# Transfers in written order, later stores, earlier weights and a ring of three for conv results in an input projection

## The chip, the cores and the metric

The kernel runs on one core of one Trainium2 chip. The metric is the device time of one execution in microseconds (us). The same executable is run three times for a median, and one more execution is profiled. Smaller is better. The engines are TensorE (PE, and PEld for its weight loads), VectorE (DVE), ScalarE (ACT), GpSimd (POOL) and SyncE (SP), which issues most of the transfers here.

## The reference

One step of a layer with two kinds of heads. 2048 prompt tokens and 8 x 8 sampled tokens go through one input projection, then through forgetting attention (8 heads of 64) and an mLSTM matrix memory (4 heads of 128), one output projection and an MLP. All is float32.

```python
z = jnp.einsum('bsd,dc->bsc', x, w_in)            # (tokens, 1024) x (1024, 3600)
fq, fk, fv, ff = ...                              # 512, 512, 512 and 8 columns of z
flogf = log_sigmoid(ff + b_fox_f)
xpad = concatenate([conv_prev, z_qk], axis=1)     # 1024 columns, mLSTM's q and k
conv = conv_b + sum(xpad[:, j:j + S] * conv_w[j] for j in range(4))
qk = silu(conv)
mv, ig, lf, og = ...                              # 512, 4, 4 and 512 columns
...
# forgetting attention: prompt over itself, sampled tokens over a paged cache
s = q . k * scale + L_q - L_k                     # L: running sum of flogf
fox_h = softmax(s) @ v
# mLSTM: chunks with a carried state C, n, m
num = (W * (q . k)) @ v + (q @ C) * a
h = num / max(|nq|, exp(-m_t))
C = g * C + sum(w_key * k * v)
...
mix = concatenate([fox_h, norm(h) * mlstm_norm_w * og]) @ w_o
x1 = layer_norm(ALPHA * x + mix)
y = layer_norm(ALPHA * x1 + square(relu(x1 @ w1)) @ w2)
```

Keys, values and log forget values of all tokens, the mLSTM's states and the conv's history are outputs too.

## The kernel before

A float32 product is made of three matmuls of split operands: high part by high, high by low, low by high (`mm3`, L144 to L149). `split_hi` (L138) makes the high part on ACT and `split_lo` (L141) the low part on DVE.

The work has four stages: the input projection (to about 1004 us) with the mLSTM and the beginning of sampled attention beside it, prompt attention (`phase_b`, L838), the output projection, and the MLP. Sampled attention goes on beside all of them.

The projection (`block_a`, L404) goes over four blocks of 512 prompt tokens; block 0 also carries the 64 sampled tokens as tile 16. A block is 14 passes over 256 columns of `w_in`: two for mLSTM's v (with the gates' 16 columns in the second), four for the conv's q and k (loop over j, L438, two j a pass), two for the output gate, and two each for attention's q, k and v. A pass is made of four units (five in block 0 where token tiles are rows of the result), each of 24 matmuls into one of four accumulators (`pm`). `wload` (L221) loads and splits a pass's weights in two halves (raw `wra`, two buffers; `whi` and `wlo`, four each). `load_x` (L256) loads one tile of 128 tokens (`xn`, two buffers), turns it on PE (L271) and splits it.

In the conv loop ACT copies two accumulators into `qi` (L456, two buffers, three columns of history in front), DVE makes four taps into `ac` (L462 and L464), ACT takes the tanh into `th` (L466), DVE combines both into `th` (L467), and SP stores `th` to `dqk` (L468). `ac`, `th` and the queries' `qst` (L522) share a ring of three buffers. Other results are copied by ACT into `st` (four buffers, L423) and stored: `dv` L429, `dog` L501, keys L536, values L541; the queries `dq` L523.

After every unit `tick` is called with an estimate of the unit's time (2.6 us, or a hundredth of the columns). It adds this to two accounts and, as they pass PACE_M (2.3) and PACE_A (7.5), advances generators, which emit a piece of other work and yield:

- `gate_stream` (L284): gates of the block's tokens, then `rowset` (L328), running sums and maxima along rows on DVE, with rows turned on PE (`mr`, L325) and stored to `dnl`, `dM`, `dar` and `dgs`.
- the prologue of sampled attention: the page table's load (L1249), four groups of cached log forget values, each of eight scans (L1301), a small matmul, eight adds (`rx`, L1311) and stores to `dR`.
- `m_block` (L606) and `m_sample` (L686): the mLSTM's chunks; `m_load_qk` (L590) loads q and k from `dqk`, the products are L631, and `norm_out` and `turn` (L553 to L574) normalise a chunk's result `hh` and store it to `dmix`. `m_sample` loads the sampled states (`C0`, L748; its matmul is L755).
- `step` (L1548) of sampled attention: `k_gather` (L1376, an indirect transfer by POOL into `kT`), `k_turn` (L1382, transposes on DVE), `r_load` (L1389, `Rb` from `dR`), `qk_step` (32 small matmuls, L1405, and a DVE reduction L1412 with `Rb`), and every 32 steps `softmax` (L1424).

The program is written in one order, and the framework places instructions on each engine's queue by its own estimates of when they are ready. Two things restrict it: the dependencies and buffers, and `issue_after`, which keeps an instruction behind a named one; `beside` (L111) uses it so that work beside the projection isn't put ahead of the projection's last issued split or matmul. SP's transfers are issued in the order in which the framework places them; a transfer that waits holds up those behind it.

The lines that block 0 and the later blocks run through:

```python
for bi in range(4):
    g = block_a(bi)
    next(g)                                   # up to the end of the conv passes
    if bi == 0 and gen:
        macc[1].append(prologue(gen))
    macc[1].append(m_block(bi))
    for _ in g:
        pass
    if bi == 0:
        while macc[1] and "pro" not in mst:
            tick(PACE_M)
        acc[1] = gen                          # sampled attention's steps
        macc[1].append(m_sample())
```

Of the kernel before, what the change touches and what calls it, by code (L numbers as in the profile page):

```python
# [24 lines left out]
D = 1024  # L25
# [25 lines left out]

@with_exitstack
def body(ctx, tc, I, O, stages):
    nc = tc.nc
    V, A, G, T, SY = nc.vector, nc.scalar, nc.gpsimd, nc.tensor, nc.sync
# [61 lines left out]

    def tick(us):

        macc[0] += us  # L120
        while macc[1] and macc[0] > PACE_M:
            macc[0] -= PACE_M
            if beside(macc[1][0]) == 0:
                macc[1].pop(0)
        if not macc[1]:
            macc[0] = 0.0
        acc[0] += us
        while acc[1] is not None and acc[0] > acc[2]:
            acc[0] -= acc[2]
            if beside(acc[1]) == 0:  # L130
                acc[1] = None
# [57 lines left out]
    def conv_setup():  # L189
        cwn = pa.tile([5, 1024], F32, name="cwn", tag="xn", bufs=2)  # L190
        SY.dma_start(cwn[0:4], I["conv_w"][0])
        SY.dma_start(cwn[4:5], I["conv_b"])
        pcw = ppa.tile([128, 8, 5], F32, name="px", tag="pm", bufs=4)
# [3 lines left out]
        scn = pa.tile([24, 1024], F32, name="scn", tag="xn", bufs=2)  # L197
        SY.dma_start(scn, I["state_conv"][0].rearrange("b j c -> (b j) c"))
# [4 lines left out]
        SY.dma_start(bog, dap(I["b_og"], 0, [[0, 128], [1, 512]]))  # L203
        SY.dma_start(nwh, dap(I["mlstm_norm_w"], 0, [[0, 128], [1, 512]]))
        V.tensor_scalar(nwh, nwh, 0.5, None, op0=OP.mult)
        SY.dma_start(smT, I["state_m"][0].rearrange("b h -> h b"))
        SY.dma_start(gbias[:, 0:8], dap(I["b_fox_f"], 0, [[0, 128], [1, 8]]))
        SY.dma_start(gbias[:, 8:12], dap(I["b_ig"], 0, [[0, 128], [1, 4]]))
        SY.dma_start(gbias[:, 12:16], dap(I["b_fg"], 0, [[0, 128], [1, 4]]))
# [11 lines left out]
    def wload(cols):  # L221

        n = sum(c[1] for c in cols)
        H, L = [], []
        for kg in range(2):
            wr = pa.tile([128, 4 * 272], F32, name="wra", bufs=2)[:, :4 * n].rearrange("p (k c) -> p k c", k=4)
            o = 0
            for c0, m in cols:
                SY.dma_start(wr[:, :, o:o + m], w_in[kg * 512:(kg + 1) * 512, c0:c0 + m].rearrange("(k p) c -> p k c", p=128))
                o += m  # L230
            wh = pa.tile([128, 4 * 272], F32R, name="whi", bufs=4)[:, :4 * n].rearrange("p (k c) -> p k c", k=4)
            wl = pa.tile([128, 4 * 272], F32R, name="wlo", bufs=4)[:, :4 * n].rearrange("p (k c) -> p k c", k=4)
            split_hi(wh, wr)
            split_lo(wl, wr, wh)
            H += [wh[:, k] for k in range(4)]
            L += [wl[:, k] for k in range(4)]
        return H, L
# [18 lines left out]
    def load_x(bi, tiles):  # L256

        blk, pre, off = geom(bi)
        for t in tiles:
            i = int(off[t] >= pre + 256)  # L260
            if len(xT.setdefault(bi, [])) == i:
                w = 256 if i else 320
                xT[bi].append((pa.tile([128, 8, w], F32R, name=f"xh{i}"), pa.tile([128, 8, w], F32R, name=f"xl{i}")))
            n = tok_n(t)
            xn = pa.tile([128, D], F32, name="xn", bufs=2)
            SY.dma_start(xn[:n], x_of(t))
            (xh, xl), s = xcol(bi, t)
            for hf in range(2):
                px = ppa.tile([128, 4, 128], F32, name="px", tag="pm", bufs=4)
                for k in range(4):  # L270
                    T.transpose(px[:, k, :n], xn[:n, (hf * 4 + k) * 128:(hf * 4 + k + 1) * 128], ident[:n, :n])  # L271
                dh = xh[:, hf * 4:hf * 4 + 4, s]
                split_hi(dh, px[:, :, :n])
                split_lo(xl[:, hf * 4:hf * 4 + 4, s], px[:, :, :n], dh)
# [9 lines left out]
    def gate_stream(bi):  # L284
# [4 lines left out]
        def gates(z, lg, shape, bb):  # L289
# [21 lines left out]
            for a, b in zip(fs, fd):  # L311
# [4 lines left out]
        SY.dma_start(O["logf_prompt"][0, 0, t0:t0 + 512].rearrange("(c p) h -> p c h", p=128),  # L316
                     gnat[:, c0:c0 + 4, 0:8])
        if pre:
            gates(gats, gnats, [64, 16], gbias[:64])
            SY.dma_start(O["logf_sample"].rearrange("l b t h -> (l b t) h"), gnats[:, 0:8])  # L320
# [7 lines left out]
        def rowset(cols, base, n_el, np_, sample):  # L328
# [35 lines left out]
            SY.dma_start(dM[:, base:base + n_el], lr)  # L364
# [12 lines left out]
            SY.dma_start(dar[:, base:base + n_el], br)  # L377
            ge = pa.tile([4, 8], F32, name="ge", bufs=1)[:, :n_el // cl]
            V.tensor_copy(ge, br.rearrange("p (c t) -> p c t", t=cl)[:, :, cl - 1])
            if sample:  # L380
                SY.dma_start(dgs_s, ge)
                me = pa.tile([4, 8], F32, name="me", bufs=1)
                V.tensor_copy(me, mr.rearrange("p (c t) -> p c t", t=cl)[:, :, cl - 1])
                SY.dma_start(mo, me)
            else:
                SY.dma_start(dgs[:, bi * 4:bi * 4 + 4], ge)
                V.tensor_copy(mend, mr[:, 511:512])
                if bi == 3:
                    SY.dma_start(O["m_prompt"].rearrange("l b h -> h (l b)"), mend)

            for i, c in enumerate(cols):
                yield 1
                s = slice(i * np_, (i + 1) * np_)
# [10 lines left out]
    def block_a(bi):  # L404
# [3 lines left out]
        def natural(sink, *cols, hook=None):  # L408
            wh, wl = first.pop() if first else wload(cols)
            for i, t in enumerate(blk):  # L410
# [7 lines left out]
                sink(t, m, ps)  # L418
                tick(2.6)
# [5 lines left out]

        for i in range(2):
# [1190 lines left out]
```

## Time and profile before

| | us |
|---|---|
| three runs, median (lowest to highest) | 3486.06 (3485.59 to 3493.94) |
| profiled execution, its time | 3461.98 |
| its span on the core | 3460.3 |
| PE busy | 3291.5, 95% |
| DVE busy | 2170.0, 63% |
| ACT busy | 1365.9, 39% |
| POOL busy | 876.3, 25% |

All times of single instructions come from the profiled execution. The profile has a page (busy time of each engine, forty slices of the span, the transfers) and views of the trace. In the windows view a row is a stretch of the span: its ends, its length, the busy time and number of instructions of each engine, the mean clock that PE was granted as a share of full speed, the busy share of the transfer engines, and GB/s. In the waits view a row names the waiting engine, its tile and line, what ended the wait, and the total time, count and longest wait in us. In the timeline a row is one instruction, or a few alike: start, duration, engine, line, operation, output and inputs, their shapes, and in brackets the idle time before it and what ended that.

### The profile page before, as it was taken

The numbers are of one execution on the slowest core, as the hardware profiler recorded it, in microseconds if no ns is written. First come the engines' busy times: TensorE is split into PE (matmuls) and PEld (weight loads), VectorE is DVE, ScalarE is ACT, GpSimd is POOL, SyncE is SP. The second block draws the span as 40 slices with busy tenths as digits, with TensorE's granted clock in tenths as the row PEclk, the third lists the DMA queues.
The fourth block names the chain that finished last, engine by engine and source line by source line (L and its number), as shares of the span: only waits on it lengthen the run. The fifth ranks groups of instructions, "written<-read, shape, count | busy, mean of one in ns | idle before, by whom it ended". The sixth has DMA issues, their size and how long they took to land.

```text
span 3460.3 us, 59595 instructions
## 1 busy us (share of the span) xinstructions
PE 3291.5 (95%) x22428; PEld 2695.6 (78%) x22428; DVE 2170.0 (63%) x5282; ACT 1365.9 (39%) x2818; POOL 876.3 (25%) x962
## 2 busy tenths in 40 slices
PE   8899999898989999999799999999999999999998
PEld 8898888887976767677577777777776777888887
DVE  4948646655658877556566667766666545755455
ACT  3333233332448888622233233332333333443332
POOL 0023122232332222266423333423333110100000
PEclk9899899999999999999899999999999999999999
DMA  5577676776772232377776866868668554442221
GB/s 172 145 211 251 190 210 220 236 240 198 240 221 79 80 82 65 108 260 264 270 241 228 278 234 239 315 208 300 243 209 296 202 179 155 153 137 74 86 86 64
DMA packets 446040, 663.16 MB, mean 192 GB/s; under 512 B 84604, under 2 KB 333760, under 8 KB 444856
## 3 DMA queue, kind: packets, MB, share of 16 engines
q1 hardware_dynamic: 369064, 380.13, 36.3%
q0 software_dynamic: 74304, 270.57, 21.3%
q10 hardware_dynamic: 2384, 8.65, 0.7%
q8 instruction: 177, 2.90, 0.3%
q14 instruction: 111, 0.91, 0.1%
HBM read 598.01 MB, written 61.22 MB: 191 GB/s over the span
## 4 chain that ended last, share of the span: by engine, by line
PE 42%; DMA 4%; issue 2%; DVE 1%; POOL 1%; ACT 0%; SPq 0%; POOLq 0%; ACTq 0%; DVEq 0%
PE py L147 7%; PE py L148 6%; PE py L149 6%; PE ph L147 6%; PE ph L148 6%; PE ph L149 6%; PE sO L1517 2%; DMA wr<-w 2%; PE sQ L1405 1%; DMA kT<-cache_k,idxK 1%; DMA vt<-cache_v,idxV 1%; PE sT L1474 1%; DVE wl L142 0%; DMA y_prompt<-y 0%; POOL kT L1376 0%
## 5 line engine op out<-in xcount | busy, mean ns | idle before, releaser
L1206 DVE TENSOR_TENSOR y<-y,py 128x512 f32<-128x512 f32 (+1 forms) x476 | 320.5, 680 | 267.8 <-PE py L149 263.7
L147 PE MATMUL ph<-x1h,wh 128*128 128x512 f32 (+1 forms) x1280 | 454.3, 355 | 6.4 <-ACT wh L139 5.1
L1382 DVE STREAM_TRANSPOSE kT<-kT 128x512 f32<-128x512 f32 x512 | 330.0, 685 | 199.2 <-DMA kT<-cache_k,idxK 198.9
L149 PE MATMUL ph<-x1h,wl 128*128 128x512 f32 (+1 forms) x1280 | 452.4, 355 | 2.1 <-DVE wl L142 2.0
L148 PE MATMUL ph<-x1l,wh 128*128 128x512 f32 (+1 forms) x1280 | 453.6, 355 | 0.0
L139 ACT ACTIVATE wh<-wr 128x1024 fp32r<-128x1024 f32 x264 | 273.0, 1056 | 439.6 <-PE py L149 232.1
L1376 POOL DMA_INDIRECT kT<-cache_k,idxK x256 | 262.1, 1024 | 715.1 <-PE sQ L1405 645.8
L147 PE MATMUL py<-wh,hh 128*128 128x512 f32 (+1 forms) x1088 | 432.3, 399 | 8.2 <-DVE y L1206 7.7
L148 PE MATMUL py<-wl,hh 128*128 128x512 f32 (+1 forms) x1088 | 427.7, 393 | 0.9 <-DVE wl L142 0.9
L149 PE MATMUL py<-wh,hl 128*128 128x512 f32 (+1 forms) x1088 | 426.6, 393 | 0.0
L142 DVE TENSOR_TENSOR wl<-wr,wh 128x1024 fp32r<-128x1024 f32 x264 | 328.4, 1249 | 90.4 <-PE ph L149 33.0
L147 PE MATMUL pm<-whi,xh 128*128 128x256 f32 (+2 forms) x1088 | 323.9, 298 | 3.5 <-DVE xl L142 2.7
L148 PE MATMUL pm<-wlo,xh 128*128 128x256 f32 (+2 forms) x1088 | 314.8, 289 | 0.0
L149 PE MATMUL pm<-whi,xl 128*128 128x256 f32 (+2 forms) x1088 | 314.1, 289 | 0.0
L147 PEld LDWEIGHTS ph<-x1h,wh 128*128 128x128 f32 x1280 | 241.7, 189 | 46.4 <-ACT wh L139 5.7
L149 PEld LDWEIGHTS ph<-x1h,wl 128*128 128x128 f32 x1280 | 241.2, 189 | 38.5 <-DVE wl L142 4.0
L148 PEld LDWEIGHTS ph<-x1l,wh 128*128 128x128 f32 x1280 | 241.5, 189 | 35.4 <-issue 2.1
L147 PEld LDWEIGHTS py<-wh,hh 128*128 128x128 f32 (+1 forms) x1088 | 201.3, 185 | 64.3 <-DVE y L1206 12.1
L149 PEld LDWEIGHTS py<-wh,hl 128*128 128x128 f32 (+1 forms) x1088 | 201.3, 185 | 50.4 <-issue 3.3
L147 PE MATMUL pm<-xh,whi 128*128 128x256 f32 (+1 forms) x768 | 227.2, 296 | 8.9 <-ACT qi L456 8.9
L148 PEld LDWEIGHTS py<-wl,hh 128*128 128x128 f32 (+1 forms) x1088 | 201.5, 185 | 43.1 <-issue 2.9
L149 PE MATMUL pm<-xh,wlo 128*128 128x256 f32 (+1 forms) x768 | 225.0, 293 | 0.0
(364 smaller groups left out, 6823.5 us busy)
## 6 DMA issues: line engine op xcount, KB each, us to landing
wr<-w SPq DMA_DIRECT2D x256, 512.0 KB
wra<-w_in SPq DMA_DIRECT2D x112, 512.0 KB
xn<-x_prompt SPq DMA_DIRECT2D x32, 512.0 KB
Rb<-dR SPq DMA_DIRECT2D x128, 128.0 KB
dqk<-th SPq DMA_DIRECT2D x32, 256.0 KB
qk<-dqk SPq DMA_DIRECT2D x16, 512.0 KB
qn<-dq SPq DMA_DIRECT2D x128, 64.0 KB
wr<-w_o SPq DMA_DIRECT2D x16, 512.0 KB
```

The source lines that it names most:

```text
L139: last["ACT"] = A.activation(dst, src, AF.Copy, scale=scale)
L142: r = (eng or V).tensor_tensor(dst, src, hi.bitcast(F32), op=OP.subtract)
L147: T.matmul(ps, wh, xh, start=first, stop=False)
L148: T.matmul(ps, wh, xl, start=False, stop=False)
L149: last["PE"] = T.matmul(ps, wl, xh, start=False, stop=stop)
L1206: V.tensor_tensor(y, y, ps, op=OP.add)
L1376: G.indirect_dma_start(out=piece(n), out_offset=None, in_=ck, in_offset=IO(ap=idxK[:, b, j // 2, j % 2:j % 2 + 1], axis=0))
L1382: V.transpose(x, x)
L1405: r = T.matmul(pq[h4 * 32:h4 * 32 + 32, hg].rearrange("p (k f c) -> p k f c", k=2, f=4), z["qb"][:, hd], kv, start=(db == 0), stop=(db == ...
L1474: T.transpose(p[:, f], z["U"][u][:, hg, f].rearrange("p k t -> p (k t)"), ident)
L1517: after_ = T.matmul(po[r:r + 32], z["PT"][:, hg, 2 * f + g, pg].rearrange("p h q -> p (h q)"), vts[f][:, g, hg * 256:(hg + 1) * 256], star ...
```

## The change

All transfers that SP issues in the input projection go through a `Lane`, which puts each behind the one written before it; this ends with the projection. Stores of results are no longer written right after the instruction that makes the result but a number of ticks later (`store`): one for `dmix`, two for most, three for the conv. Weights of a pass are loaded (`w_load`) during the pass two before it and split (`w_split`) during the pass before. Rows of x are loaded (`x_load`) apart from their turning (`x_turn`). The conv writes its tanh and its result in place of its input, `qi`, which has three buffers and which `qst` uses too; `ac` has two of its own and isn't stored. The q and k of the next chunk are loaded at p = 0 instead of p = 1, and at a block's beginning ahead of the chunk's other loads. `Rb` gets a second buffer (the place comes from `qr`, which moves into the tag of `vt`), and the softmax of a sampled sequence stands one to two steps later. Each engine has as many instructions as before.

```diff
+class Lane:
+    def __init__(self, tc):
+        self.tc, self.held, self.at = tc, True, None
+
+    def dma_start(self, *a):
+        if not self.held:
+            return self.tc.nc.sync.dma_start(*a)
+        with ExitStack() as es:
+            if self.at is not None:
+                es.enter_context(self.tc.issue_after(self.at))
+            r = self.tc.nc.sync.dma_start(*a)
+        self.at = r.ins
+        return r
...
-    V, A, G, T, SY = nc.vector, nc.scalar, nc.gpsimd, nc.tensor, nc.sync
+    V, A, G, T, SY = nc.vector, nc.scalar, nc.gpsimd, nc.tensor, Lane(tc)
...
+    def begin(every=False):
+        for e in list(late):
+            e[0] -= 1
+            if every or e[0] <= 0:
+                late.remove(e)
+                e[1]()
+
+    def store(n, dst, src):
+        later(n, lambda: SY.dma_start(dst, src))
+
     def tick(us):
+        begin()
...
+    def weights():
+        W["at"] += 1
+        return W["parts"].pop(W["at"])
+
+    def ahead(u):
+        p = W["at"]
+        if u < 2:
+            w_split(p + 1, u)
+        if 1 <= u < 3:
+            w_load(p + 2, u - 1)
...
-            SY.dma_start(dnl[:, base:base + n_el], fr)
             ir = R[0][0:4, 0:n_el]
             yield 1
+            SY.dma_start(dnl[:, base:base + n_el], fr)
...
-            wh, wl = first.pop() if first else wload(cols)
+            wh, wl = weights()
             for i, t in enumerate(blk):
...
                 sink(t, m, ps)
+                ahead(i)
                 tick(2.6)
...
-                SY.dma_start(dv[r:r + m, i * 256:(i + 1) * 256], stage(ps[:, :256], m, 256))
+                store(2, dv[r:r + m, i * 256:(i + 1) * 256], stage(ps[:, :256], m, 256))
...
-            qi = pa.tile([128, 515], F32, name="qi", bufs=2)
+            qi = pa.tile([128, 515], F32, name="qi", bufs=3)
...
-                tick(w * 0.01)
...
                 A.copy(qi[:, 3 + i * 256:259 + i * 256], ps[:, w - 256:])
+                ahead(j % 2 * 2 + i)
+                tick(w * 0.01)
...
-                ac = pa.tile([128, 512], F32, name="ac", tag="ac", bufs=3)[:, :n]
+                ac = pa.tile([128, 512], F32, name="ac", bufs=2)[:, :n]
...
-                th = pa.tile([128, 512], F32, name="th", tag="ac", bufs=3)[:, :n]
                 A.activation(th, ac, AF.Tanh)
                 V.scalar_tensor_tensor(th, th, 1.0, ac, op0=OP.add, op1=OP.mult)
-                SY.dma_start(dst, th)
+                store(3, dst, th)
-            conv(lambda q: qi[:, q:q + 512], dqk[j, :, t0:t0 + 512], 512)
+            conv(lambda q: qi[:, q:q + 512], dqk[j, :, t0:t0 + 512], qi[:, 0:512])
...
-            st = pa.tile([128, 512], F32, name="qst", tag="ac", bufs=3)
+            st = pa.tile([128, 515], F32, name="qst", tag="qi", bufs=3)[:, :512]
...
-            SY.dma_start(dmv[:, 4:8, tok0:tok0 + np_], ot[:, :, :np_])
+            store(1, dmv[:, 4:8, tok0:tok0 + np_], ot[:, :, :np_])
...
+        begin(True)
+        qk = m_load_qk(bi * 4)
+        yield 1
+        yield 1
+        va, Wm, qa = m_load(bi * 4)
         gsb = pm.tile([128, 4, 4], F32, name="gsb", bufs=2)
         SY.dma_start(gsb, dap(dgs, bi * 4, [[0, 128], [16, 4], [1, 4]]))
-        qk = m_load_qk(bi * 4)
-        va, Wm, qa = m_load(bi * 4)
...
-                if p == 1 and c % 4 < 3:
+                if p == 0 and c % 4 < 3:
                     qk = m_load_qk(c + 1)
...
-    load_x(0, [16])
-    first = [wload([(C_V, 256)])]
-    load_x(0, [0])
+    x_load(16, 0)
+    for p in range(2):
+        for kg in range(2):
+            w_load(p, kg)
+            if p == 0:
+                w_split(p, kg)
+    x_turn(0, 16)
+    x_load(1)
+    x_turn(0, 0)
+    x_load(2)
...
+    begin(True)
+    SY.held = False
...
-        rb = state[b]["rb"] = ps_.tile([128, 2, 256], F32, name="Rb", bufs=1)
+        rb = state[b]["rb"] = ps_.tile([128, 2, 256], F32, name="Rb", bufs=2)
...
             after = qk_step(g)
-            if g % 8 == 7:
-                softmax(g // 8)
+        b = at(n, 35, 32)
+        if b is not None and b < 8:
+            softmax(b)
...
-        b = at(n, 35, 32)
+        b = at(n, 37, 32)
         if b is not None and b < 8:
             softmax_new(b)
             v_new(b)
-        b = at(n, 39, 32)
+        b = at(n, 40, 32)
         if b is not None and b < 8:
             softmax_sum(b)
```

More of the change, by code (lines that the diff above doesn't have):

```diff
@@ L116, in beside, with later @@
             return next(gen, 0)
+    late = []
+    def later(n, f):
+        late.append([n, f])
+    def begin(every=False):
[6 more added lines that the diff above has]
+        later(n, lambda: SY.dma_start(dst, src))
     def tick(us):
+        begin()
         macc[0] += us
@@ L219, in body @@
     mend = pa.tile([4, 1], F32, name="mend")
[L221 to L237, printed above, removed]
+    PASSES = 4 * ([[(C_V, 256)], [(C_V + 256, 256), (C_FF, 8), (C_I, 8)]]
+                  + [[(C_QK + i * 256, 256)] for i in range(4)]
+                  + [[(c + i * 256, 256)] for c in (C_O, 0, 512, 1024) for i in range(2)])
@@ new lines, in body, with w_load, w_split @@
+    W = dict(raw={}, parts={}, at=-1)
+    def w_load(p, kg):
+        if p >= len(PASSES):
+            return
+        n = sum(c[1] for c in PASSES[p])
+        wr = W["raw"][p, kg] = pa.tile([128, 4 * 272], F32, name="wra", bufs=2)[:, :4 * n].rearrange("p (k c) -> p k c", k=4)
+        o = 0
+        for c0, m in PASSES[p]:
+            SY.dma_start(wr[:, :, o:o + m], w_in[kg * 512:(kg + 1) * 512, c0:c0 + m].rearrange("(k p) c -> p k c", p=128))
+            o += m
+    def w_split(p, kg):
+        if p >= len(PASSES):
+            return
+        wr = W["raw"].pop((p, kg))
+        n = wr.shape[2]
+        wh = pa.tile([128, 4 * 272], F32R, name="whi", bufs=4)[:, :4 * n].rearrange("p (k c) -> p k c", k=4)
+        wl = pa.tile([128, 4 * 272], F32R, name="wlo", bufs=4)[:, :4 * n].rearrange("p (k c) -> p k c", k=4)
+        split_hi(wh, wr)
+        split_lo(wl, wr, wh)
+        H, L = W["parts"].setdefault(p, ([], []))
+        H += [wh[:, k] for k in range(4)]
+        L += [wl[:, k] for k in range(4)]
```

147 lines of the change are left out of this document (86 added, 61 removed).

## The prediction

> **What bounds the kernel now.** I read the page first, then the span cut at the borders of the stages (the input projection ends at about 1004 us), then what PE waited for in each cut, and last the timeline around the longest waits.
>
> ```profile
> PEclk9899899999999999999899999999999999999999
> ...
> wra<-w_in SPq DMA_DIRECT2D x112, 512.0 KB
> xn<-x_prompt SPq DMA_DIRECT2D x32, 512.0 KB
> ```
> ```profile
> core 0: us, PE busy (x) PEld busy (x) DVE busy (x) ACT busy (x) POOL busy (x), PEclk, DMA share, GB/s
> 0.00:50.00 50.00, 38.81 (x280) 37.96 (x280) 15.58 (x31) 17.14 (x27) 5.19 (x14) 0.97 0.71 221
> 50.00:190.00 140.00, 124.71 (x936) 121.45 (x935) 114.03 (x370) 44.48 (x97) 16.03 (x14) 0.93 0.56 159
> 190.00:250.00 60.00, 58.03 (x470) 57.82 (x470) 23.71 (x71) 21.41 (x49) 10.75 (x14) 0.94 0.64 185
> 250.00:400.00 150.00, 136.00 (x1174) 123.76 (x1174) 119.87 (x306) 44.25 (x86) 38.80 (x49) 0.94 0.70 224
> 400.00:990.00 590.00, 546.78 (x4774) 509.79 (x4774) 344.46 (x936) 204.37 (x456) 151.06 (x172) 0.96 0.70 219
> 1015.00:3461.00 2446.00, 2371.10 (x14715) 1831.96 (x14713) 1542.13 (x3528) 1028.04 (x2086) 643.22 (x680) 0.99 0.55 184
> ```
>
> PE is busy nearly everywhere, so the change can win only what PE loses in the projection. PE's idle time is the stretch less its busy time: 11.2, 15.3, 2.0, 14.0 and 43.2 us in the first five rows. Besides that, PEclk below 1 there means that PE ran some of its matmuls at half speed. A stretch at half clock lasts about 2 x (1 - PEclk) x length: 19.6, 7.2, 18.0 and 47.2 us in rows two to five, of which half is lost where PE is busy. The waits of PE (us in total, times, longest us), first in 50 to 250, then in 400 to 990:
>
> ```profile
> PE px L481 <- ACT qi L456: 6.8, 1, 6.8
> PE mr L325 <- DVE rows L332: 5.1, 1, 5.1
> ...
> PE pm L147 <- ACT qi L456: 0.9, 1, 0.9
> PE px L481 <- ACT cs_n L482: 0.7, 1, 0.7
> ```
> ```profile
> PE sQ L1424 <- DVE mxs L1412: 12.5, 1, 12.5
> PE px L271 <- DMA xn<-x_prompt: 8.4, 2, 6.7
> PE mm L631 <- DMA qk<-dqk: 7.9, 2, 6.5
> PE mm L755 <- DMA C<-state_C: 3.6, 2, 3.1
> PE mm L631 <- DVE st L498: 3.1, 1, 3.1
> ```
>
> None is for split weights. Behind the longest stands the ring of the conv results; DVE's and ACT's waits up to 1015 us, and the end of the projection's last conv:
>
> ```profile
> DVE ac L462 <- DMA dqk<-th: 27.0, 8, 13.8
> ```
> ```profile
> ACT th L466 <- DMA dqk<-th: 15.0, 2, 11.2
> ```
> ```profile
> 853.82 0.55 DVE L462 TENSOR_SCALAR ac<-qi,cw 128x512 f32<-128x512 f32 x1 [13.78 <-DMA dqk<-th]
> 855.21 0.61 PE L1424 MATMUL sQ<-qt,qb 128*32 128x8 f32 x32 [12.47 <-DVE mxs L1412]
> ```
>
> DVE stood 13.78 us before a conv, because ac, th and qst share three buffers and the one it needs was still being stored. The score reduction queued behind it on DVE came late, and PE's softmax matmuls waited 12.47 us for that; they started 1.4 us after that conv.
>
> **The change, part by part.** Instructions are as many as before; buffers and order differ. Effects are in us, minus for faster.
>
> Conv ring, loads and stores in blocks 1 to 3 (400 to 990): **-41**. ac is no longer stored, and a store of qi has three conv units until its buffer comes again. So the 13.78 us on DVE fall away and the 12.5 on PE with them: what is late next is nothing I can find, since the reduction then follows its matmuls as it does elsewhere. The chunk's q/k load now stands one unit earlier (at the first half of the chunk, p = 0) and ahead of the weight rows, so 7.9 and 3.1 go to nothing; between load and use lie over 100 matmuls, 11.5 us at the row's 546.78/4774 = 0.1145 us. The load itself takes 5.7, by a transfer of the same size:
>
> ```profile
> 517.16 0.88 SPq L266 DMA_DIRECT2D xn<-x_prompt  x1
> 522.84 1.94 PE L271 MATMUL px<-ident,xn 128*128 128x128 f32 x8 [6.69 <-DMA xn<-x_prompt]
> ```
>
> Issue to use is 5.68. In the changed order 37 to 46 matmuls, 4.2 to 5.3 us, stand between a row load of x and its transposes. That leaves 0.4 to 1.4 us in each of three blocks, so I keep 4 of the 8.4. State_C now has 96 matmuls (11 us) between load and both uses, against 61 and 103 before; 1 of 3.6 stays. Gain in idle: 12.5 + 11.0 + 4.4 + 2.6 = 30.5. If every stretch at half clock fell on a busy PE, 23.6 us would be lost here; part falls into the waits, so I take 15, and give back the same share as of the idle time: 15 x 30.5/43.2 = 10.6. Bounds: -58 (all of 43.2 and 15) and -18, with the 12.5 moved elsewhere and half of the 10.6 kept.
>
> Block 0 (50 to 250): **-9**. The four waits shown, 6.8 + 5.1 + 0.9 + 0.7 = 13.5, follow DVE's and ACT's waits on the ring and go. But sampled attention's prologue is moved: its page table load is now behind six conv stores in SP's queue, and its four groups fall among the projection's later units, with 25 matmuls (2.9 us) between neighbours.
>
> ```profile
> 147.43 2.03 DVE L1311 TENSOR_SCALAR rx<-ri,sf 128x128 f32<-128x128 f32 x8
> 151.06 2.28 DVE L1301 TENSOR_TENSOR_SCAN ri<-onesr,lg 128x128 f32<-128x128 f32 x7
> ```
>
> A group costs DVE 2.6 (eight scans) + 2.03 + about 0.4 for two copies = 5.0 us, and rx has one buffer that its own store holds. So 2.1 us a group stick out: 8.5. Net idle is -5.0 of 17.3, and of the 13.4 that half clock can cost here the same share, 3.9, comes back. Bounds: -24 (no group is waited for, and 10.5 of the clock comes back) and +18 (each group pays 5.0 and a landing of 5.7 against its 2.9).
>
> Between block 0 and 1 (250 to 400): **+14**. Sampled attention has fallen behind by then and about twenty of its steps are issued together. In the changed PE order three score steps (L1405) stand in a row, with at most three other matmuls between. Each needs keys gathered into a ring of three that the step before frees:
>
> ```profile
> 294.02 0.96 POOL L1376 DMA_INDIRECT kT<-cache_k,idxK  x1 [6.26 <-PE sQ L1405]
> 304.16 1.93 PE L1405 MATMUL sQ<-kT,qb 128*32 128x256 f32 x32
> 306.40 0.96 POOL L1376 DMA_INDIRECT kT<-cache_k,idxK  x1 [1.32 <-DVE kT L1382]
> 317.26 1.93 PE L1405 MATMUL sQ<-kT,qb 128*32 128x256 f32 x32
> ```
>
> Gather to scores takes 10.1 and 10.9 us; here units of the projection filled it, there two such cycles stand open: 20.2. Behind that, in written order, weights wait for the gate stream's dnl store and Rb for softmax:
>
> ```profile
> SPq L429 <- ACT st L423: 68.3, 27, 8.8
> ...
> SPq L1389 <- DVE mxs L1412: 34.6, 9, 11.4
> ```
>
> Two such waits at the last row's mean of 3.8 make 7.6. 20.2 + 7.6 - 14.0 = 13.8. Bounds: +4 (one cycle covered) and +26 (a third open cycle of 10.9, and a little of the clock).
>
> Start (0 to 50): **+2**. The third row load is now queued behind the second pass's weights, and these wait for the first split.
>
> ```profile
> 8.56 1.23 DVE L142 TENSOR_TENSOR wlo<-wra,whi 128x1024 fp32r<-128x1024 f32 x1 [0.45 <-ACT whi L139]
> 20.25 1.94 PE L271 MATMUL px<-ident,xn 128*128 128x128 f32 x8 [2.61 <-DMA xn<-x_prompt]
> ```
>
> Its issue falls behind 8.56 + 1.23 = 9.8, its landing at 15.5 at the earliest, with two weight loads ahead; the later wait of 2.61 can go. Bounds -2.6 and +5.7.
>
> End (990 to 1015): **+2**. The prompt attention's first load, which POOL and PE wait for, now follows the last dmix store:
>
> ```profile
> 999.30 0.39 SPq L865 DMA_DIRECT2D dup<-k_prompt  x1
> ...
> 1000.95 0.37 SPq L574 DMA_DIRECT2D dmix<-ot  x1
> ```
>
> 1.65 + 0.37 = 2.0, between 0 (dmix comes earlier too) and that.
>
> After 1015: **0**. Written order ends here; Rb has two buffers and softmax comes a step later. PE is idle only 75 of 2446 us. Bounds -10 and +10, about one wait like the 12.5 either way.
>
> A second look at the clock:
>
> ```profile
> 186.00:190.00 4.00, 2.11 (x19) 1.89 (x17) 2.08 (x6) 1.42 (x3) 2.33 (x2) 1.00 1.07 308
> 190.00:194.00 4.00, 4.00 (x23) 4.00 (x23) 0.21 (x1) 1.53 (x6) 0.63 (x1) 0.57 0.98 270
> ```
>
> After 1.89 us of idle, PE ran four busy us at 0.57, with 23 matmuls where 35 fit. [...]
>
> **The sum**: 2 - 9 + 14 - 41 + 2 + 0 = **-32** against the profiled execution's 3461.98: about 3430. The three runs' median, 3486.06, is 24 above it, and I let that difference stand: 3486.06 - 32 = **3454**.
>
> **Rivals.**
> *Weights late (slower).* Each weight load now waits until all written before it is issued: evictions (up to 8.8 us, row above) and Rb (11.4). A load is written three units, 24 matmuls each, before its split: 8.2 us, and 5.7 of them go to landing. What is left, 2.5 us, and two free accumulators, 5.5, cover 8.0. The 11.4 alone oversteps this by 3.4, and two shorter waits in a row add up likewise. For it: ACT runs its splits and evictions in one queue. Against it: stores are now written two units late, so the 68.3 us of waiting should shrink, and
>
> ```profile
> ACT whi L139 <- DMA wra<-w_in: 23.0, 7, 6.2
> ```
>
> ACT already waits for weights, up to 6.2 us, with no PE wait behind it. At 1 us a pass (an overstep of 3.4 in every third pass or so) over the 54 passes that follow the first two it costs 54: 3454 + 54 = 3508. It decides from 0.8 us a pass: 54 x 0.8 = 43 outweighs the 32 and 10.5 more.
>
> *The waits only move (no change).* For it: DVE is busy 114.03 of 140 and 119.87 of 150, and there nothing late can be made up. Against it: in 400 to 990 it is busy 344.46 of 590. With half of the 41 kept, and block 0 at nothing: 2 + 0 + 14 - 20 + 2 = -2, so 3484.
>
> *More is won.* If the three steps find their keys early, +14 becomes +4, and if 400 to 990 loses only 5 of its 43.2: 2 - 9 + 4 - 53 + 2 = -54, with -10 after 1015: 3422. For it: SP issues nothing early that blocks a later urgent load. Against it: DVE's kT and dn groups still end waits in that stretch.
>
> *It does not do what it says.* Only the projection's transfers are bound to written order; where the old order was already the written one, nothing moves. The list of SP's transfers differs throughout, so I give this nothing of its own.
>
> **How the numbers follow.** 3454 has 0.52, late weights 0.20, moved waits 0.14, more won 0.14. The likeliest case's own range is 3436 to 3474, from half of the bounds' width, since they will not all fall one way. 3 runs of this kernel lie 8.35 apart, and about 0.3%, 10.5 us, can be told from no change: faster means below 3475.6, slower above 3496.5. Faster: 0.50 + 0.14 = 0.64; within: 0.02 + 0.12 = 0.14; slower 0.20 and 0.02 of the moved waits = 0.22. The range reaches from the larger gain to the middle of the late weights' case: 3418 to 3503.
>
> **What would show it.** DVE's wait of ac on dqk's store is gone, and PE's 12.5 at the softmax matmuls too. PE waits for the q/k load vanish in 400 to 990, and PEclk there is 0.97 to 0.98. In 250 to 400, three score steps with two gaps of 8 to 11 us, POOL gathers between. PE waits at L183 or its neighbours for whi or wlo would mean the weights' case; so would ACT's waits for wra above 23.0 us in total with PE idle behind them. It would be wrong if idle time in 400 to 990 stays above 30 us, or if the run loses more after 1015 than before.

## The result and the profile after

The changed kernel takes 3523.84 us (median of 5 runs, 3521.06 to 3526.57) against 3486.59 for the kernel before (median of 5, 3485.59 to 3493.94): a ratio of 1.0101, 95% interval 1.0086 to 1.0116. It is 37 us slower (35 by the ratio) where 32 us faster was forecast, and outside the range.

Its profiled execution took 3523.84, too. The profiled execution of before, 3461.98, lay below all its timed runs, so the two traces lie 62 us apart where the kernels lie 37 apart. Times are compared by ratios to runs of before on the same chip in what follows (before's median was 3465 to 3490 us, by the chip); the traces say where a loss is, and to some 10 us how large.

The windows of the changed kernel, cut as before (stretch, its length, busy time and count of PE, PEld, DVE, ACT and POOL, clock, transfer share, GB/s):

```profile
0.00:50.00 50.00, 34.57 (x262) 34.04 (x263) 15.05 (x30) 15.97 (x26) 0.77 (x10) 1.00 0.54 164
50.00:190.00 140.00, 118.76 (x882) 115.48 (x881) 102.57 (x337) 36.95 (x79) 10.41 (x11) 0.95 0.49 135
190.00:250.00 60.00, 51.92 (x400) 50.94 (x401) 24.71 (x72) 22.15 (x52) 11.77 (x15) 0.89 0.70 198
250.00:400.00 150.00, 109.39 (x930) 97.66 (x929) 84.06 (x227) 34.66 (x71) 41.82 (x47) 0.87 0.61 181
400.00:990.00 590.00, 548.44 (x4739) 509.77 (x4740) 359.88 (x974) 204.37 (x447) 148.46 (x162) 0.96 0.71 222
```

PE's idle time by stretch is 15.4, 21.2, 8.1, 40.6 and 41.6 us, against 11.2, 15.3, 2.0, 14.0 and 43.2. Almost all the loss of idle time stands before 400 us, 26.6 of it in 250 to 400. From 400 to 990, where 30.5 of idle time were to go, 1.6 went.

A stretch of time holds other work in each kernel, so here is the projection cut by work as well. Block 0 ends with the last of its 1536 matmuls into `pm`, block 1 after 1344 more, and the projection with the first transpose of prompt attention (us, from PE's instructions in the traces; the runs e2 to e14 follow below):

| | block 0 | block 1 | blocks 2 and 3 | end of the projection |
|---|---|---|---|---|
| before | 263.6 | 251.2 | 489.7 | 1004.5 |
| before, second profile (e5) | 258.5 | 255.5 | 484.7 | 998.7 |
| changed | 279.4 | 283.0 | 491.9 | 1054.3 |
| e2, sampled attention free | 277.2 | 255.6 | 503.5 | 1036.3 |
| e3, no written order | 252.4 | 255.0 | 496.4 | 1003.8 |
| e4, only the conv's buffers | 252.9 | 257.4 | 493.8 | 1004.1 |
| e6, weights free | 254.7 | 273.0 | 473.7 | 1001.4 |
| e11, weights and Rb free | 255.6 | 253.8 | 493.2 | 1002.5 |
| e14, only beside work bound | 247.6 | 256.5 | 476.2 | 980.4 |

Two traces of one kernel differ by up to about 5 us in the first two columns and by up to 11 in the third.

The two waits that the change was to remove are in the lists no more: that of DVE's `ac` for its store, and the 12.5 us at the softmax. But DVE now waits for stores from the new ring of `qi`, 14.1 us as below and 4.5 for `dqk`, where it had waited 27.0 (up to 1060 us):

```profile
DVE qi L523 <- DMA dq<-qst: 14.1, 3, 10.6
```

PE waits 15.0 us for split weights (L182 for ACT's `whi`: 6.8, 5.5 and 2.7 in three stretches). Far more shows on ACT, up to 1050 us (total, count, longest):

```profile
ACT whi L174 <- DMA wra<-w_in: 190.8, 58, 43.4
```

Before, this row read 23.0, 7 and 6.2. What stood ahead of the weights is seen in SP's own waits over the same stretch:

```profile
SPq L64 <- ACT st L493: 149.5, 51, 9.8
SPq L64 <- DVE rows L404: 51.9, 4, 24.7
SPq L64 <- DVE n L890: 31.2, 3, 16.1
...
SPq L64 <- DVE rows L430: 30.5, 4, 11.0
```

The first are evictions of the projection, the others the gate stream's rows and the sampled states, work beside it. The longest run of SP held by one kind of transfer is that of the Rb loads behind block 0. SP's timeline there:

```profile
304.36 33.21 SPq L64 DMA_DIRECT2D Rb<-dR  x10
337.61 0.59 SPq L64 DMA_DIRECT2D wra<-w_in  x1
```

ACT's timeline:

```profile
347.92 1.06 ACT L174 ACTIVATE whi<-wra 128x1024 fp32r<-128x1024 f32 x1 [43.37 <-DMA wra<-w_in]
348.88 0.35 ACT L493 COPY st<-pm 128x256 f32<-128x256 f32 x1
```

And PE's, for the waits between score steps:

```profile
331.76 1.07 PE L1511 MATMUL sQ<-kT,qb 128*32 128x256 f32 x7 [10.11 <-DVE kT L1488]
345.68 1.93 PE L1511 MATMUL sQ<-kT,qb 128*32 128x256 f32 x16 [10.28 <-DVE kT L1488]
```

Read together: Rb has two buffers, so SP stands until the score steps free them (24.3 us of its waits here are for DVE's `mxs`, L1518). The next pass's weights are behind, issued at 337.61. ACT has their split at the head of its queue and does nothing for 43 us, and behind the split wait the evictions of accumulators that PE has filled. Yet this longest wait costs PE little. PE runs no matmul of the projection from 318.3 to 351.6 us because three score steps stand in a row in its own queue and each waits for its keys; the wait for weights behind them is 2.8 us. In e6, where no split waits more than 3.9 us for weights, the same steps hold PE nearly as long, from 294.5 to 325.7:

```profile
307.40 3.45 PE L1511 MATMUL sQ<-kT,qb 128*32 128x256 f32 x32 [9.97 <-DVE kT L1488]
322.13 3.64 PE L1511 MATMUL sQ<-kT,qb 128*32 128x256 f32 x32 [11.28 <-DVE kT L1488]
```

So most of what late weights cost lies elsewhere: by the table, e6 is 24.7 us shorter than the changed kernel in block 0, 10.0 in block 1 and 18.2 in blocks 2 and 3.

### The profile page after: what moved, and what is told of

Its sections match the earlier page's. It is cut to its first block, busy times and chain, and to the rows that moved or that the text cites. A ratio compares the mean times of both kernels' runs of the same rounds, so it can differ in the third digit from the quotient of the medians.

```text
span 3522.2 us, 59510 instructions
## 1 busy us (share of the span) xinstructions
PE 3305.7 (94%) x22428; PEld 2692.0 (76%) x22428; DVE 2157.8 (61%) x5282; ACT 1365.8 (39%) x2818; POOL 895.6 (25%) x962
## 4 chain that ended last, share of the span: by engine, by line
PE 40%; DMA 4%; issue 3%; DVE 2%; POOL 1%; ACT 1%; another core or an unknown queue 0%; SPq 0%; POOLq 0%; ACTq 0%; DVEq 0%
PE py L182 6%; PE py L184 6%; PE py L183 6%; PE ph L184 6%; PE ph L182 6%; PE ph L183 6%; DMA wr<-w 2%; PE sO L1623 2%; PE sQ L1511 1%; DVE wl L177 1%; DMA kT<-cache_k,idxK 1%; PE sT L1580 0%; DVE kT L1488 0%; DVE y L1312 0%
## 5 line engine op out<-in xcount | busy, mean ns | idle before, releaser
L182 PE MATMUL ph<-x1h,wh 128*128 128x512 f32 (+1 forms) x1280 | 454.6, 356 | 4.1 <-ACT wh L174 2.5
L182 PE MATMUL py<-wh,hh 128*128 128x512 f32 (+1 forms) x1088 | 432.4, 399 | 11.6 <-DVE y L1312 9.1
L182 PE MATMUL pm<-whi,xh 128*128 128x256 f32 (+2 forms) x1088 | 320.1, 295 | 18.2 <-ACT qi L535 6.3
L182 PEld LDWEIGHTS ph<-x1h,wh 128*128 128x128 f32 x1280 | 241.3, 189 | 45.0 <-issue 6.9
L182 PEld LDWEIGHTS py<-wh,hh 128*128 128x128 f32 (+1 forms) x1088 | 201.0, 185 | 72.7 <-DVE y L1312 14.6
L182 PE MATMUL pm<-xh,whi 128*128 128x256 f32 (+1 forms) x768 | 228.4, 298 | 11.4 <-ACT whi L174 6.5
L177 DVE TENSOR_TENSOR wlo<-wra,whi 128x1024 fp32r<-128x1024 f32 (+1 forms) x112 | 139.2, 1244 | 149.7 <-ACT whi L174 149.0
```

What stands on the lines that cost most here:

```text
L177: r = (eng or V).tensor_tensor(dst, src, hi.bitcast(F32), op=OP.subtract)
L182: T.matmul(ps, wh, xh, start=first, stop=False)
```

## The experiments

Each time is a median with its ratio to before on the same chip. Waits are ACT's for raw weights up to 1050 us.

**e1: without the run of steps.** Written order, no run of about twenty sampled steps.

```diff
-            acc[1] = gen
+            acc[0], acc[1] = 0.0, gen
```

> The account that advances sampled attention's steps is set to zero when the steps begin, so the run of about twenty steps written at once behind block 0 is gone; all else as in the changed kernel. Theory 1 (the written order turns that run of steps into the loss: three score steps in a row on PE and ten Rb loads, 33 us of SP, ahead of the next weights): PE idle in 250 to 400 us falls from 40.6 to at most 15, and the time from 3524 to 3475-3485. Theory 2 (written order is late everywhere, the run of steps is only where it shows most): ACT's waits for raw weights stay over 120 of their 190.8 us up to 1050, and the time is 3505-3520.

3512.29 us, 1.0060 (1.0042 to 1.0079); waits 124.3, longest 7.3. Idle time in 250 to 400 fell to 5.1, better than theory 1 asked for, and the projection ended at 964 us instead of 1054. The time fell by only 14 us (1.0101 to 1.0060), as theory 2 had it. The trace shows why the two don't match: 192 of the 608 score matmuls are no longer beside the projection, and what follows it takes 2551 us instead of 2468.

**e8: the same on the kernel before**, to separate the moved steps from the order.

> The kernel before with the run of about twenty steps of sampled attention taken away in the same manner as in e1. In e1 the projection ended 40 us earlier than in the first profile of before and the whole was still 25 slower: Theory A (the twenty steps are done later, where they cost 50 to 65 us): the projection ends 30 to 45 us earlier and the time is 3500-3515. Theory B (they cost little later, and e1 lost by its order after the projection): the time is 3450-3470.

3475.36, 1.0017 (1.0000 to 1.0034): the projection ends 46 us earlier than in e5, and 76 us are lost after it. Theory A in mechanism, though 6 us slower instead of 32 or more. Taken away by itself, the run of steps gains nothing. With it away in both kernels, written order and all else still cost 15 us (1.0060 against 1.0017), so 20 of the 35 need the run and the order together.

**e2: sampled attention out of the written order** (it gets the plain queue in place of the `Lane`).

```diff
-        gen = sample_attention(tc, I, O, ps_, pps, cst, ident, sqk, dnl, dR, dmix, dqb, vx, SY)
+        gen = sample_attention(tc, I, O, ps_, pps, cst, ident, sqk, dnl, dR, dmix, dqb, vx, nc.sync)
```

> Only sampled attention's transfers (page table, dR, dqb, bn, Rb) are taken out of the written order; the rest of the projection stays in it, and the run of steps stays. Theory 1: the score steps are again 70 to 100 matmuls apart on PE, the 20 us of waits for keys go, and so does most of block 0's second half (33 us), as the prologue's groups stand early again: 3460-3475. Theory 2 (the other stores hold the weights up): 3500-3515.

3506.9, 1.0064 (1.0043 to 1.0084); waits 151.3. The score steps are apart, the 20 us of waits are gone and block 1 takes 255.6 us instead of 283.0, but blocks 2 and 3 take 11.6 longer, about as much as two traces can differ, and block 0 keeps its loss. It is theory 2's time: score steps in a row weren't the main loss.

**e3: no written order at all.**

```diff
-        self.tc, self.held, self.at = tc, True, None
+        self.tc, self.held, self.at = tc, False, None
```

> No transfer is bound to written order; ring of three, late stores, early weights and the rest stay. Theory 1 and 2 alike: the order was all that was lost, 3450-3470, with ACT's waits for raw weights back near 23 us. Rival (the ring and the early weights are worth nothing by themselves, waits move): 3480-3495.

3474.76, 0.9966 (0.9951 to 0.9981), and on another chip as e17

> The kernel of e3 (no written order) again on the chip of e16. If order of the beside work is worth something by itself, e16 is 15 to 35 faster than this one, which stands 8 to 18 below before; if not, both are within 10 of each other.

3471.47, 0.9951 (0.9927 to 0.9975). Waits 18.5 and 12.6. By these ratios the order turned a gain of 12 to 17 us into a loss of 35.

**e4: only the conv's buffers**, on the kernel before.

```diff
-            qi = pa.tile([128, 515], F32, name="qi", bufs=2)
+            qi = pa.tile([128, 515], F32, name="qi", bufs=3)
...
-                ac = pa.tile([128, 512], F32, name="ac", tag="ac", bufs=3)[:, :n]
+                ac = pa.tile([128, 512], F32, name="ac", bufs=2)[:, :n]
```

> The kernel before with only the conv's new buffers (ac two, tanh and result in place of the input, qi three, shared with the queries). The prediction's step: DVE's 27.0 us of waits for the conv store and PE's 12.5 at the softmax go, 25 to 45 us faster than before: 3442-3461. Rival (waits only move): 3478-3490.

3480.19, 0.9970 (0.9956 to 0.9983): 10 us, inside the rival's range. In its waits of DVE, of ACT, and of PE in 400 to 990, the store that held `ac` now holds `qi`, and the wait at the softmax shrinks to 3.0 while 9.2 and 8.8 appear next to it:

```profile
DVE qi L443 <- DMA dqk<-qi: 27.8, 7, 7.0
```
```profile
ACT qi L456 <- DMA dqk<-qi: 47.1, 10, 12.3
```
```profile
PE sT L1454 <- ACT Sn L1444: 9.2, 1, 9.2
PE pm L147 <- ACT qi L456: 8.8, 2, 8.4
...
PE sQ L1424 <- DVE mxs L1412: 3.0, 1, 3.0
```

**e5: the kernel before, profiled again.**

> The kernel before, profiled a second time, since its first profiled execution (3461.98) lies below all of its timed runs so far (3477.99 to 3500.74). Both theories: a span of 3478 to 3495. Theory A (the missing 16 to 30 us lie in the projection): PE idle in 400 to 990 us is over 55. Theory B (they lie after 1015 us, beside the MLP, where transfers of sampled attention meet the weights): the projection ends within 3 us of 1004 and 2446 us of the first profile become 2462 or more.

3452.96 on a chip where before's runs were 3456.78 to 3483.86 (median 3468.2): again a profiled execution at the low end. Neither theory A nor B: the projection ended at 998.7, and 2452.6 us followed.

**e6: raw weights out of the written order**, all else in it.

```diff
-            SY.dma_start(wr[:, :, o:o + m], w_in[...])
+            nc.sync.dma_start(wr[:, :, o:o + m], w_in[...])
```

> The changed kernel with only the raw weights' loads taken out of the written order. Theory 1 (weights come late because each is behind stores and Rb): ACT's waits for raw weights fall from 190.8 to below 60 and the time from 3524 to 3485-3500; the three score steps in a row stay, with their 20 us. Theory 2 (what is lost is lost in the other loads and in PE's order): 3510-3525, whatever ACT waits.

3450.79, 0.9951 (0.9934 to 0.9968): from 1.0101, 1.5% or 52 us, more than theory 1 had said, and faster than before. Its waits, and its two windows from 250 on:

```profile
ACT whi L174 <- DMA wra<-w_in: 21.8, 14, 3.9
```
```profile
250.00:400.00 150.00, 106.54 (x899) 94.50 (x898) 100.01 (x258) 36.22 (x70) 36.17 (x43) 0.85 0.59 183
400.00:990.00 590.00, 565.81 (x5021) 528.82 (x5020) 361.95 (x988) 212.42 (x472) 167.08 (x182) 0.98 0.73 232
```

From 400 to 990 PE idles 24.2 us instead of 41.6, at a clock of 0.98 instead of 0.96. From 250 to 400 it idles 43.5, as the score steps still stand in a row. Up to the end of the projection its idle time is 100.3 us, against 137.0 in the changed kernel and 92.3 in before. From 400 to 990 PE's waits begin with:

```profile
PE px L340 <- DMA xn<-x_prompt: 14.9, 2, 8.2
```

**e7: late stores out of the written order.**

```diff
-        later(n, lambda: SY.dma_start(dst, src))
+        later(n, lambda: nc.sync.dma_start(dst, src))
```

> The changed kernel with the late stores taken out of the written order, loads kept in it. Theory 1a (stores that wait for their data block the weights): ACT's waits for raw weights fall below 100, time 3490-3505. Theory 1b (loads block loads: Rb and the mLSTM's ahead of the weights): 3510-3522, waits for raw weights over 130.

3486.39, 1.0050 (1.0032 to 1.0068); waits 144.5. 18 us (1.0101 to 1.0050), a third of what e6 gives: neither 1a nor 1b alone; both stores and other transfers stand ahead of the weights.

**e9 and e10: weights a unit earlier, and a unit later**, in written order.

```diff
-        if 1 <= u < 3:
-            w_load(p + 2, u - 1)
+        if u < 2:
+            w_load(p + 2, u)
```

> The changed kernel, all in written order, with each raw weight load written one unit of 24 matmuls earlier (directly behind the split that frees its buffer). Theory 1 (a load has 8.2 us from where it is written to its split, and what stands ahead of it in SP's queue takes more): a third of the lateness goes, ACT's waits for raw weights fall from 190.8 to 100-140 up to the end of the projection, and the time, which stood 35 above before, stands 10-25 above it. Rival (the weights block others when they stand early: SP waits for the split's end with the rest behind it): 35-50 above.

> As e9, but each raw weight load written one unit later. Theory 1: 2.75 us less for each of 54 passes' two halves, ACT's waits for raw weights rise above 280 us and the time stands 70-120 above before. Rival (only a few long waits of SP matter, a shift by one unit is nothing): 30-45 above.

3519.21, 1.0099 (1.0082 to 1.0116), waits 144.0, longest 42.2; and 3529.03, 1.0120 (1.0099 to 1.0141), waits 204.8. One unit moved ACT's waits by -47 and +14 us and the time by nothing that stands out from the intervals. Theory 1's arithmetic of a unit more or less for every load is wrong. The one long wait doesn't decide either: e9 keeps it, e10's longest is 15.2, and e10 isn't the faster.

**e11 and e12: e6, and besides it Rb's loads, or the rows of x, out of the order.**

> As e6 (raw weights out of the written order, 17 faster than before), and Rb's loads out of it too. The three score steps then stand 65 to 100 matmuls apart on PE instead of in a row. Theory C (the two gaps of 10.0 and 11.3 us between score steps in e6 are lost time): both fall below 4, and the time stands 28-38 below before. Rival (the matmuls that filled the gaps were only moved; keys come no sooner): 12-22 below.

> As e6, and x's row loads out of the written order too. In e6 PE waits 14.9 us for x rows in 400 to 990, in before 8.4. Theory D (rows are held up by the stores and weights written ahead of them): these waits fall below 5 and the time stands 22-30 below before. Rival (rows land late because their buffers come free late): waits over 10, 12-20 below.

3475.78, 0.9968 (0.9953 to 0.9984), and 3477.21, 0.9975 (0.9964 to 0.9987). In e11 one gap of 5.1 is left of the two between score steps and nothing is won; in e12 PE's waits for x are 8.4 instead of 14.9 and nothing is won either. By work, e11's block 1 is 19.2 us shorter than e6's and its blocks 2 and 3 are 19.5 longer. The gaps were lost time in block 1, and as much was lost later in their place; why isn't shown.

**e13 and e14: only the projection's own transfers in written order, and only those beside it.** In e13 `Lane` is off while a generator is advanced, in e14 it is on only then.

```diff
-            return next(gen, 0)
+            was, SY.held = SY.held, False
+            try:
+                return next(gen, 0)
+            finally:
+                SY.held = was
```

> The changed kernel with everything that is issued while a generator is advanced beside the projection (gate stream, mLSTM, sampled attention with its ten Rb loads) out of the written order; weights, rows of x and the projection's late stores stay in it. Theory H (a few long holds by beside work stand ahead of the weights: in the changed kernel's trace up to 1055 us SP waited 51.9 + 30.5 us for the gate stream's rows, 31.2 for the sampled states, 24.3 for Rb's buffer): ACT's waits for raw weights fall below 70 of 190.8 and the time stands 5 to 20 below before. Theory S (the projection's own evictions, 149.5 us of waits, stand ahead of the weights): waits over 120, 15 to 35 above before.

> The reverse of e13: only what is issued beside the projection is bound to written order, among itself; weights, rows of x and late stores are free of it. No weight stands behind a hold in written order. Theories H and S alike: ACT's waits for raw weights below 40, 5 to 20 below before. Rival (the order of the beside work costs by itself, through late mLSTM and sampled loads): 5 to 25 above before.

e13: 3459.16, 0.9989 (0.9972 to 1.0007), waits 88.1, longest 8.4. e14: 3426.02, 0.9886 (0.9850 to 0.9923), waits 10.3. e13 is close to theory H: with the beside work's holds away, waits are halved and 39 us (1.0101 to 0.9989) come back, three quarters of what e6 gives; that the late stores hold the rest agrees with e7's 18. e14 is the fastest version, 40 us below before where 5 to 20 were expected; why it is so much isn't settled. It and the changed kernel were run once more, with e17 above on the same chip:

> The changed kernel again, beside e16 and e17 on one chip, since the kernel before took 3464 to 3488 us on the chips so far. If the loss belongs to the kernel, it stands 30 to 42 above before here too (1.0086 to 1.012). If it depends on the chip, under 20.

> The kernel of e14 again: 25 to 50 below before if its 0.9886 holds on another run, 5 to 20 below if that was the state of one chip.

e15: 3525.71, 1.0122 (1.0079 to 1.0166). e16: 3459.82, 0.9931 (0.9908 to 0.9955). The intervals against before overlap with e17's (0.9951, 0.9927 to 0.9975), but the two ran on one chip and can be compared directly: seven runs of 3452.0 to 3467.6 us against ten of 3461.8 to 3488.6, medians 11.7 us apart. That lies between the two expectations. The order of the beside work gains something here, but not the 28 us between e14 and e3, which were on two chips.

Waits and ratios together: 204.8 (e10, 1.0120), 190.8 (changed, 1.0101), 151.3 (e2, 1.0064), 144.5 (e7, 1.0050), 144.0 (e9, 1.0099), 124.3 (e1, 1.0060), 88.1 (e13, 0.9989), 23.5 and less (e6, e11, e12, e3, e14: 0.9886 to 0.9975). e9 stands out of the line, and e1 a little, whose moved steps cost 6 us in e8.

## Why the prediction was wrong

**The step that failed is the one that cost the weights at nothing.** "Weights late" was written down as a rival with a chance of 0.20 and a price of 54 us. e6 measures its price: 52 us by the ratios, and 52.9 by the ends of the projection. That 54 is so near is luck: it was 1 us for each of 54 passes, from an overstep "in every third pass or so" that no row gives, and the loss isn't spread that way (24.7 us stand in block 0 alone). The rival was set aside by three arguments, and each was wrong.

*Cover.* A load was to have 8.0 us before PE feels it, and an overstep of 3.4, the longest old wait of 11.4 less 8.0, was put in every third pass. That two waits in a row add up was said, and not counted. The ten Rb loads alone held SP 33.21 us with the weights behind. In before they came in pairs (296.54, 309.70, 324.53 us and so on) with weight loads issued between them. The longest wait in the old trace was no bound for the new order.

*Late stores.* "Stores are now written two units late, so the 68.3 us of waiting should shrink." Before, three lines of evictions waited 68.3, 57.7 and 54.6 us (the last two, L541 and L536, in the same list as the first); after, their common line waits 149.5 of that 180.6. Two units later in the program isn't two units later than the eviction. ACT's waits for weights explain only a small part of that: in e6, where they are 21.8 us, the row of the stores still reads 126.9.

*ACT waits for weights without a PE wait behind.* This was a misreading of before's own trace. Behind the longest of these waits, 6.19 us, stands PE's longest wait between 250 and 400 us, a stretch whose waits the prediction doesn't list. PE stood still from 342.04 on, 7.62 us, for an eviction that came behind the split in ACT's queue. ACT's two rows, then PE's:

```profile
347.77 1.06 ACT L139 ACTIVATE whi<-wra 128x1024 fp32r<-128x1024 f32 x1 [6.19 <-DMA wra<-w_in]
349.25 0.62 ACT L456 COPY qi<-pm 128x256 f32<-128x256 f32 x2
```
```profile
349.66 0.58 PE L147 MATMUL pm<-xh,whi 128*128 128x256 f32 x1 [7.62 <-ACT qi L456]
```

So a late weight stops PE under the name of an eviction. PE's list of the changed kernel names the weights with 15.0 us, and e6 gives back 52; its idle time up to the end of the projection falls by 36.7 of that, the rest is busy time. A long wait of ACT isn't always paid, though: the 43.4 us lie beside the score steps, which PE waited for anyway.

**The terms of the sum**, as far as the traces tell them:

- Start, +2: +2.4 by ACT's fourth eviction (34.6 against 32.2), and as much by the 240th matmul into `pm` (52.5 against 50.1). Right.
- Block 0, -9: it ends 15.8 us later, at 279.4. Without any order (e3) and with the conv's buffers alone (e4) it ends at 252.4 and 252.9, 6 to 11 us earlier than before's 258.5 and 263.6, so the term holds there. e6's 254.7 says less, since its start is 5 us earlier than before's.
- 250 to 400, +14: idle time rose by 26.6, just above the upper bound of 26. The two open cycles were there (10.11 and 10.28 us, 20.2 predicted), but besides them PE had 20.2 us of other waits instead of 7.6. By work, block 1 takes 273 to 288 us in the versions where sampled attention's loads share one order with the projection's transfers (changed, e6, e7, e9, e10, e12), and 251 to 258 in the others (without e1 and e8, which have fewer steps there). How much of it is lost in the end isn't settled: e11 closed most of the gaps and won nothing.
- 400 to 990, -41: this term, the largest of the sum, failed too. 1.6 of 30.5 idle us went in the changed kernel. The waits for q/k and the softmax went as said, but others came: 7.3 us of a transpose behind DVE's `dn`, 6.1 for the sampled states, where 1 was to stay, and 5.5 for ACT's `ot`. In e6 idle time fell by 19.0 in this stretch (43.2 to 24.2), with the rows of x at 14.9, where 4 were to stay, but it rose before 400 us. By work, blocks 1 to 3 take 740.9 and 740.2 us in before's two traces, 746.7 in e6, 751.4 in e3, 751.2 in e4 and 732.7 in e14: no version shows the sum of this term and the last, -27. Mostly the waits moved, as the rival of that name had it.
- The clock's part of it, -10.6: half clock is seen in before's trace (PEclk 0.50 from 190.5 to 193.5 us, where matmuls of 128x256 start 0.21 us apart; from 194 on, at 1.00, 0.12). Time at half clock by 2 x (1 - PEclk) x length fell from 47.2 us to 23.6 in e6, 11.8 lost where PE is busy. Against e5, whose PEclk there is 0.97 (35.4 us), it is 5.9. So before's two traces don't tell the 10.6 from little more than half of it. What makes the clock fall was not shown by any run.
- After 1015, 0: 2467.8 us followed the projection, against 2455.8 in before's first trace; so 12 of the 62 us between the traces stand here. On chips where before takes 3487 to 3490 us this part took 2460 to 2472 in all versions (but e1), on those where it takes 3464 to 3468, 2442 to 2453 (but e8). No effect of the change was separated from that.
- Two ranges don't come out of their own terms: half of the clock's 10.6 kept puts the bound of 400 to 990 at -23, not -18, and half of the summed bounds' width gives 3425 to 3492, not 3436 to 3474. Neither reaches 3524.

**The gain was forecast too large, and where it lies isn't shown.** By the runs, the change gains 17 us without the weights in order (e6), 12 to 17 without any order (e3, e17), and the conv buffers alone 10 (e4). 32 was reached only by e14 (0.9886, 40 us), not by the same kernel on another chip (e16, 0.9931, 24 us). In the traces the projection ends at 1001.4 us in e6, 1003.8 and 1007.9 in e3 and e17 and 1004.1 in e4, about where before's two traces have it (1004.5 and 998.7); only e14 and e16 end clearly earlier, at 980.4 and 990.3. Before's two profiled executions lie 24 and 15 us below its medians, so its traces don't show what its usual execution loses, and the gains of 10 to 17 us have no place yet. Of the 67 us between the forecast of -32 and the 35 lost, 52 are the weights; the other 15 are gain that didn't come.

## What to carry to other kernels

Transfers in written order are only as early as the latest one ahead of them (ten Rb loads held the weights behind them for 33.2 us), so what an engine's queue head needs soon (here weights for a split with evictions behind it) shouldn't share an order with stores and ring loads that wait for slow work. When an edit binds an order, add up all waits that can now stand in a row, and don't take the longest single wait of the old trace as a bound. For each long wait of the engine that empties the accumulators, look at what PE does in the same microseconds: 6.2 us on ACT cost PE 7.6 in before, and 43.4 lay beside waits that PE had anyway. And compare two traces by work done, not by stretches of time, before a gap is called a loss or a gain.

## What had not been expected

With e14's split of the order, raw weights, rows and stores of the projection placed freely and only the beside work bound, the kernel is faster than before by 0.7% to 1.1% (0.9931 and 0.9886), the best of all versions.

In e1 and e8 the projection ends 90 and 46 us earlier and the kernel gains 14 or loses 6: about twenty steps of sampled attention taken away from the projection cost 76 to 83 us later. An end of a stage is no measure where work can move out of it.

The kernel before has medians from 3464.5 to 3489.7 us on the chips that ran it. The difference seems to lie mostly after the projection: 2452.6 us in e5, where its median was 3468.2, and 2467 to 2472 in e3, e4, e11 and e12 on chips where it was 3487.6 and 3487.7, with as many instructions to do. But these are other kernels, and before's own first trace has 2455.8 us at a median of 3486, so this isn't shown.
